# Modulation vectors of the first block: products on ScalarE in place, plain adds on VectorE, the bias row on GpSimd

## The chip, the cores and the metric

The kernel runs on one core of a Trainium2 chip. The core has five engines that matter here: TensorE (PE: matmuls and transposes; PEld is its weight load), VectorE (DVE), ScalarE (ACT), GpSimd (POOL) and SyncE (SP), which only issues DMAs. Each engine takes its instructions from one queue, in order; engines wait for one another by semaphores. The metric is the device time of one execution in microseconds.

## The reference, cut to what matters

The program is two transformer blocks of two layers each, on 512 tokens of width 1024. The change lies in the first block, which has two layers that are modulated by a condition vector `c` (1 x 1024):

```
c_act = silu(c)
for l in range(2):
    mod = c_act @ w_mod[l] + b_mod[l]                 # 1 x 3072, w_mod[l]: 1024 x 3072, f32
    shift, scale, gate = split(mod, 3)                # 1024 each
    h = rms_norm(x, pre_gain[l]) * (1 + scale) + shift
    proj = h @ w_in[l]                                # then attention, retention and gated linear attention (GLA)
    y = concat(attention, retention, gla) @ w_out[l]
    x = x + gate * rms_norm(y, post_gain[l])
```

So each layer needs three vectors of 1024. The scale and shift of layer 0 are needed at once. Its gate is needed only at the end of layer 0, scale and shift of layer 1 at the start of layer 1, and the gate of layer 1 at its end. These four vectors are the ones that the change touches.

## The kernel before, in words

Matmuls of the projections are done in three passes over a weight tile that is split in a rounded and a remaining part: `load_w` (L211 on) loads 128x512 f32 into one of four `raw` buffers by a DMA on SP (L213), ACT casts it (L226), DVE subtracts (L227), and PE multiplies three times (L231 to L233, `mm3`). The four weight buffers are free again when PE has passed. Loads, casts and subtractions of weights thus keep PE's pace.

A vector is made in `mod_steps(l, i)` (L356), a generator that is pulled along beside other work. It treats two halves of 512 columns. For one half it loads the bias (one row, L365) and eight chunks of `w_mod`, 128x512 f32 or 256 KB each (L368), all by SP and all into one ring of two buffers (`rawm`, the bias row included). `mod_acc` (L385) multiplies each chunk by one scalar per partition (column k of `ca`) and adds it up in the tile `acc`, of which there is one: k = 0 is a product (L387) and the addition of the bias row on one partition (L388), k = 1 to 7 are one fused multiply and add each (L390), all on DVE. Then `late`, put off by four steps, lets PE add up the 128 partitions by a matmul with a matrix of ones (L375) and spreads the result over all partitions, and ACT (L377) or DVE (L379, L381) puts it in its place. `acc` is free for the next half when this matmul has read it.

In layer 0, `finish_layer` chains six halves (gate 0, scale 1, shift 1) as `bg`; in layer 1 two (gate 1). `bg` is pulled in the loop over the seven GLA levels (L727), and woven into the GLA chain (L790), the retention chain (L876) and the attention (L1018). The GLA levels: L700 to L704 make the decays `d` of a level on DVE, ACT and POOL, PE multiplies (L669, L679), and DVE selects from the product into `Sg` (L725). The GLA chain: PE multiplies (L781, L783), the norm and gate of its result run on ACT (L543), DVE (L545 to L555) and POOL (L281, L282), PE transposes it (L274), and ACT and DVE split it (L246, L247). Beside it run the projections that `dD` pulls; their rotation is on DVE (L531 to L538) and its transposes on PE (L744).

The first two vectors of layer 0 are made by another function, `mod0` (L416), which calls `mod_acc` too, and which the change leaves alone.

The order in each engine's queue is not the order in the text: a scheduler of the framework places the instructions by its own estimates of times. A change of one operation therefore moves others.

Of the kernel before, what the change touches and what calls it, by code (L numbers as in the profile page):

```python
# [14 lines left out]
OP = mybir.AluOpType  # L15
# [106 lines left out]
def _body(ctx, tc, nc, a, out, stop):  # L122
    V, SC, GP, PE = nc.vector, nc.scalar, nc.gpsimd, nc.tensor
# [30 lines left out]
    def ps_mm():  # L154
        return psum("mm", [128, 512], 4)
# [128 lines left out]
    def bcast_row(dst, row):  # L284
        n = row.shape[-1]
        nc.sync.dma_start(dst, bass.AP(tensor=row.tensor, offset=row.offset, ap=[[0, 128], [1, n]]))
# [22 lines left out]
    def later(steps, fn, key=None):  # L309
        pend.append((clock[0] + steps, fn, key))  # L310
# [31 lines left out]
    def first_block():  # L342
# [5 lines left out]
        ca = fp.tile([128, 8], F32, name="ca")  # L348
# [7 lines left out]
        def mod_steps(l, i):  # L356
            t_ = md.tile([128, D], F32, name=f"mod{i}", bufs=1)
            mod[l][i] = t_
            if i:
                bcast_row(t_, (a["pre_norm_gain"] if i == 1 else a["post_norm_gain"])[l])  # L360
            for n in range(0, D, 512):
                c0 = D * i + n
                acc = md.tile([128, 512], F32, name="acc", bufs=1)
                br = md.tile([128, 512], F32, tag="rawm", name="br", bufs=2)[0:1]
                nc.sync.dma_start(br, a["b_mod"][l:l + 1, c0:c0 + 512])  # L365
                for k in range(8):
                    raw = md.tile([128, 512], F32, tag="rawm", name="rawm", bufs=2)
                    nc.sync.dma_start(raw, a["w_mod"][l, 128 * k:128 * k + 128, c0:c0 + 512])  # L368
                    mod_acc(acc, raw, br, k)
                    if k < 7:  # L370
                        yield 1

                def late(dst=t_[:, n:n + 512], src=acc):
                    ps = ps_mm()
                    PE.matmul(ps, ones, src, start=True, stop=True)  # L375
                    if i == 0:
                        SC.copy(dst, ps)  # L377
                    elif i == 1:
                        V.scalar_tensor_tensor(dst, ps, 1.0, dst, op0=OP.add, op1=OP.mult)  # L379
                    else:  # L380
                        V.tensor_tensor(dst, ps, dst, op=OP.mult)  # L381
                later(RT['mdl'], late, "mod")
                yield 1

        def mod_acc(acc, raw, br, k, eng=V):  # L385
            if k == 0:
                eng.tensor_scalar(acc, raw, ca[:, 0:1], None, op0=OP.mult)  # L387
                eng.tensor_tensor(acc[0:1], acc[0:1], br, op=OP.add)  # L388
            else:
                eng.scalar_tensor_tensor(acc, raw, ca[:, k:k + 1], acc, op0=OP.mult, op1=OP.add)  # L390

        def norm(l, t, x, pl):
# [5 lines left out]
            for n in range(2):  # L398
# [5 lines left out]
        sil = ([fp.tile([128, 512], F32, name=f"sil_a{t}") for t in range(4)],  # L404
               [fp.tile([128, 256], F32, name=f"sil_r{t}") for t in range(4)])
        Ks = [dict(mod=mod[l], sil=sil, mod_steps=mod_steps, norm=norm, md=md) for l in range(2)]
        load_E, mm_E, ev_E = start_layer(0, Ks[0])
        nst = ExitStack()
# [1679 lines left out]
    if SKIP_FIRST:  # L2088
        tst = ExitStack()
        nc.sync.dma_start(con, a["con"])  # L2090
        nc.sync.dma_start(con2, a["con2"])
        tp = pool("tp", stack=tst)
        drain(bias_steps(tp))
        wst = ExitStack()
        more_w("wx", 10, wst, "right")
        E = start_even()
        for t in range(4):
            xt = tp.tile([128, D], F32, name="xt", bufs=2)
            nc.sync.dma_start(xt, xd[t])
            to_T(hT, 0, t, xt, 8)  # L2100
        for t in (3, 2, 1, 0):
            drain(E(t))
        wst.close()
        tst.close()
    else:
        first_block()
# [61 lines left out]
```

## Time and profile before

| | |
|---|---|
| runs of the kernel | 1941.02, 1931.21, 1941.77 us; median 1941.02 |
| profiled execution | 1936.26 us, of which the span of the trace is 1934.5 |
| mean granted TensorE clock in it | 0.992 of full speed |
| PE busy | 1874.2 us, 97% of the span |
| DVE, ACT, POOL busy | 1251.6, 828.1, 260.1 us (65%, 43%, 13%) |
| DMA | 218.76 MB, 113 GB/s in the mean |

All times below are of this one profiled execution. Busy time of an engine counts its instructions, waits left out; idle time of an engine counts only where another engine waits for it. In rows of single instructions the first number is the start in microseconds from the begin of the span, the second the duration, and the brackets hold how long the engine stood idle just before and for which instruction or DMA it waited. A row can hold several like instructions in sequence (x2, x3). PE executes a matmul of f32 in two records. The granted clock is a share of full speed (2.4 GHz; the lower level, 1.2 GHz, is 0.5).

### The profile page before, as it was taken

What the parts mean: (1) busy time and instruction counts of PE and PEld (TensorE: products, weight loads), DVE (VectorE), ACT (ScalarE), POOL (GpSimd) and SP (SyncE); (2) the same over time, 40 slices, a digit from 0 to 9 for tenths busy, and PEclk for the clock granted to TensorE, in tenths of its full rate; (3) what the DMA queues carried; (4) which work ended last, traced back from release to release, by engine and by line L of the source; (5) the groups of instructions that cost most, each with busy time, mean ns of one, the idle gap of its engine ahead of it and who ended that gap; (6) DMA issues with size and microseconds to landing.
All of it is one profiled execution on the core that took longest, in us unless ns stands there. A gap on an engine that the chain in (4) does not pass through costs nothing.

```text
span 1934.5 us, 29305 instructions
## 1 busy us (share of the span) xinstructions
PE 1874.2 (97%) x10144; PEld 1518.6 (79%) x10144; DVE 1251.6 (65%) x3060; ACT 828.1 (43%) x1840; POOL 260.1 (13%) x380
## 2 busy tenths in 40 slices
PE   7899899999999999999999999999999999999997
PEld 4777687877888888868888888788778888888886
DVE  5697886485775244686675674755776776756646
ACT  2432354433463344453443443244665544434341
POOL 3011101012101000101020020101441200200101
PEclk9999999999999999999999999999999999999999
DMA  8535524226124233403373362363114033733632
GB/s 278 173 89 165 150 86 137 86 84 183 44 94 157 73 106 121 153 12 116 117 155 99 91 149 72 117 188 91 42 29 148 24 133 112 154 97 96 134 88 82
DMA packets 139784, 218.76 MB, mean 113 GB/s; under 512 B 21633, under 2 KB 53747, under 8 KB 139636
## 3 DMA queue, kind: packets, MB, share of 16 engines
q1 hardware_dynamic: 130420, 200.11, 33.6%
q0 software_dynamic: 9216, 16.78, 5.2%
q8 instruction: 80, 1.31, 0.3%
q14 instruction: 68, 0.56, 0.1%
HBM read 207.20 MB, written 14.09 MB: 114 GB/s over the span
## 4 chain that ended last, share of the span: by engine, by line
PE 65%; DVE 7%; issue 6%; POOL 3%; DMA 2%; ACT 1%; POOLq 0%; DVEq 0%; SPq 0%; ACTq 0%
PE mm L1060 10%; PE mm L1062 10%; PE mm L1061 9%; PE mm L231 6%; PE mm L233 6%; PE mm L232 6%; PE t L1095 1%; PE o L1547 1%; PE o L1549 1%; PE o L1548 1%; DMA bq<-in_ffn_w_down_dram 1%; PE mm L1547 1%; PE mm L1549 1%; PE mm L1548 1%; PE t L274 1%
## 5 line engine op out<-in xcount | busy, mean ns | idle before, releaser
L227 DVE TENSOR_TENSOR w<-raw,w 128x512 fp32r<-128x512 f32 (+4 forms) x496 | 307.5, 638 | 140.1 <-ACT w L226 138.4
L226 ACT CAST w<-raw 128x512 fp32r<-128x512 f32 (+4 forms) x504 | 284.5, 575 | 239.8 <-PE mm L233 55.9
L1060 PE MATMUL mm<-hT,w 128*128 128x512 f32 x920 | 366.6, 399 | 0.2
L1062 PE MATMUL mm<-hT,w 128*128 128x512 f32 x920 | 361.6, 394 | 0.1
L1061 PE MATMUL mm<-hT,w 128*128 128x512 f32 x920 | 360.7, 392 | 0.0
L231 PE MATMUL mm<-w,hT 128*128 128x512 f32 (+3 forms) x704 | 278.3, 396 | 1.4 <-ACT hT L243 1.3
L233 PE MATMUL mm<-w,hT 128*128 128x512 f32 (+3 forms) x704 | 262.5, 373 | 0.4 <-DVE hT L244 0.4
L232 PE MATMUL mm<-w,hT 128*128 128x512 f32 (+3 forms) x704 | 261.0, 371 | 0.1
L1060 PEld LDWEIGHTS mm<-hT,w 128*128 128x128 f32 x920 | 172.9, 188 | 39.7 <-ACT w L226 1.8
L1062 PEld LDWEIGHTS mm<-hT,w 128*128 128x128 f32 x920 | 172.7, 188 | 39.4 <-DVE w L227 1.3
L1061 PEld LDWEIGHTS mm<-hT,w 128*128 128x128 f32 x920 | 172.9, 188 | 35.2
L231 PEld LDWEIGHTS mm<-w,hT 128*128 128x128 f32 x704 | 138.9, 198 | 31.0 <-issue 6.5
L233 PEld LDWEIGHTS mm<-w,hT 128*128 128x128 f32 x704 | 138.8, 197 | 21.9 <-DVE hT L244 1.3
L232 PEld LDWEIGHTS mm<-w,hT 128*128 128x128 f32 x704 | 139.4, 198 | 16.8 <-issue 2.0
L1525 POOL DMA_DIRECT2D bq<-in_ffn_w_down_dram x64 | 56.6, 1280 | 413.0 <-DVE w L244 401.7
L1576 DVE SCALAR_TENSOR_TENSOR g<-mm,cw,g 128x511 f32<-128x511 f32 x44 | 33.0, 749 | 108.5 <-ACT g L1575 108.4
L243 ACT CAST w<-bq 128x512 fp32r<-128x512 f32 x112 | 69.0, 621 | 65.1 <-DMA bq<-in_ffn_w_down_dram 20.2
L1090 ACT ACTIVATE E<-E,nm 128x128 f32<-128x128 f32 (+3 forms) x128 | 71.6, 560 | 45.0 <-DVE nm L1089 42.3
L244 DVE TENSOR_TENSOR w<-bq,w 128x512 fp32r<-128x512 f32 x112 | 75.5, 689 | 15.4 <-ACT w L243 14.8
L1582 DVE TENSOR_TENSOR ge<-ge,mm 128x512 f32<-128x512 f32 x44 | 30.1, 685 | 67.6 <-PE mm L1062 67.5
L1575 ACT ACTIVATE g<-mm,cw 128x512 f32<-128x512 f32 x44 | 34.2, 777 | 79.6 <-PE mm L1062 63.1
L1085 DVE COPY pT<-t 128x512 f32<-128x512 f32 (+3 forms) x84 | 43.0, 512 | 37.8 <-PE t L1280 23.3
(472 smaller groups left out, 3458.3 us busy)
## 6 DMA issues: line engine op xcount, KB each, us to landing
raw<-in_ffn_w_up_dram SPq DMA_DIRECT2D x160, 256.0 KB
rawm<-in_w_mod_dram SPq DMA_DIRECT2D x96, 256.0 KB
raw<-in_w_in_dram SPq DMA_DIRECT2D x80, 256.0 KB
bq<-in_ffn_w_down_dram POOLq DMA_DIRECT2D x64, 256.0 KB, 7.7
raw<-in_ev_w_in_dram SPq DMA_DIRECT2D x48, 256.0 KB
bq<-in_ffn_w_down_dram SPq DMA_DIRECT2D x48, 256.0 KB
raw<-in_w_out_dram SPq DMA_DIRECT2D x32, 256.0 KB
raw<-in_ffn_w_down_dram SPq DMA_DIRECT2D x24, 256.0 KB
```

Source lines behind the costliest of these rows:

```text
L226: SC.copy(hi, r)
L227: (eng or V).tensor_tensor(lo, r, hi.bitcast(F32), op=OP.subtract)
L231: PE.matmul(ps, hi, w[:, 0, w0:w0 + n], start=first, stop=False)
L232: PE.matmul(ps, hi, w[:, 1, w0:w0 + n], start=False, stop=False)
L233: PE.matmul(ps, lo, w[:, 0, w0:w0 + n], start=False, stop=last)
L243: SC.copy(hi, ps)
L244: V.tensor_tensor(lo, ps, hi.bitcast(F32), op=OP.subtract)
L1060: PE.matmul(ps, wh, hi, start=k == ks[0], stop=False)
L1061: PE.matmul(ps, wh, lo, start=False, stop=False)
L1062: PE.matmul(ps, wl, hi, start=False, stop=k == ks[-1])
L1090: SC.activation(E, E, AF.Exp, scale=scale, bias=nm, accum_out=den)
L1525: GP.dma_start(bufs[name, p], src[then](p), accum_op=OP.add)
```

## The change

`mod_steps` calls a new function, `mod_acc_split`. For k = 0 ACT multiplies the chunk into `acc`, and POOL adds the bias row to its first partition. For k = 1 to 7 ACT multiplies the chunk in place, in its load buffer, and DVE adds it to `acc`. Buffers, loads and the final matmul are the same. `mod_acc` stays for `mod0`.

```diff
-                    mod_acc(acc, raw, br, k)
+                    mod_acc_split(acc, raw, br, k)
...
+        def mod_acc_split(acc, raw, br, k):
+            if k == 0:
+                SC.mul(acc, raw, ca[:, 0:1])
+                GP.tensor_tensor(acc[0:1], acc[0:1], br, op=OP.add)
+            else:
+                SC.mul(raw, raw, ca[:, k:k + 1])
+                V.tensor_tensor(acc, acc, raw, op=OP.add)
```

In the changed kernel all lines from L392 of the old one on have a number that is 8 higher; L387, L388, L390 and L391 are the four operations of the new function there.

The scheduler moves work at several places. On SP, at the beginning of the third half of layer 0 (h3), the queue of the kernel before reads (`br` is the bias row, `rawm` a chunk of `w_mod`, `raw` a weight tile of the projection):

```order
L365 DMA br<-in_b_mod_dram 1x512
L368 DMA rawm<-in_w_mod_dram 128x512
L213 DMA raw<-in_w_in_dram 128x512 x2
L368 DMA rawm<-in_w_mod_dram 128x512 x2
L213 DMA raw<-in_w_in_dram 128x512 x3
L368 DMA rawm<-in_w_mod_dram 128x512 x2
```

and that of the changed kernel:

```order
L365 DMA br<-in_b_mod_dram 1x512
L213 DMA raw<-in_w_in_dram 128x512 x3
L368 DMA rawm<-in_w_mod_dram 128x512
L213 DMA raw<-in_w_in_dram 128x512 x3
L368 DMA rawm<-in_w_mod_dram 128x512 x2
L213 DMA raw<-in_w_in_dram 128x512 x2
```

The first chunk has moved behind three weight loads, the second behind six.

On ACT, in the fourth half (h4), beside the end of the GLA chain, the kernel before has (L246 is the copy of a transposed GLA result, L745 that of a transposed key of the retention):

```order
L246 ACTIVATE yT<-t,ggain 128x2x128
L226 CAST w<-raw 128x512 x4
L246 ACTIVATE yT<-t,ggain 128x2x128
L745 COPY rkT<-t 128x2x128 x2
L226 CAST w<-raw 128x512 x4
```

and the changed kernel (L753 is the old L745):

```order
L387 ACTIVATE acc<-rawm,ca 128x512
L390 ACTIVATE rawm<-rawm,ca 128x512 x2
L246 ACTIVATE yT<-t,ggain 128x2x128
L226 CAST w<-raw 128x512 x4
L246 ACTIVATE yT<-t,ggain 128x2x128
L390 ACTIVATE rawm<-rawm,ca 128x512 x2
L753 COPY rkT<-t 128x2x128
```

The products of k = 0 to 2 stand ahead of the copies and casts, those of k = 3 and 4 behind them. At the end of the second half (h2), the product of k = 7 stands behind four casts in the same way.

On PE, the L375 of h3 has in the kernel before two of four L783 of a GLA result ahead of it:

```order
L274 MATMUL t<-con,ng 128x128 x2
L781 MATMUL o<-smk_1551,qe 128x256
L783 MATMUL o<-v_589,Sg 128x64 x2
L375 MATMUL mm<-acc,ones 128x512
L231 MATMUL mm<-w,hT 128x512
```

and in the changed kernel all of the GLA results and a transposed key (L789, L791 and L752 are the old L781, L783 and L744):

```order
L274 MATMUL t<-con,ng 128x128 x2
L789 MATMUL o<-smk_1571,qe 128x256
L791 MATMUL o<-v_589,Sg 128x64 x4
L789 MATMUL o<-smk_1572,qe 128x256
L274 MATMUL t<-con,ng 128x128 x2
L791 MATMUL o<-v_590,Sg 128x64 x4
L752 MATMUL t<-con,rk_1485 128x128 x2
L375 MATMUL mm<-acc,ones 128x512
```

Eleven short instructions have moved ahead of L375. The L375 of h2 has moved in the same way, behind 18 matmuls of 256 columns (and two transposes) that followed it; that of h4 keeps its place.

## Rows read from the trace of the kernel before

**Rows 1.** The page, first part: busy us, share of the span, instructions.
```profile
PE 1874.2 (97%) x10144; PEld 1518.6 (79%) x10144; DVE 1251.6 (65%) x3060; ACT 828.1 (43%) x1840; POOL 260.1 (13%) x380
```

**Rows 2.** PE's waits in 100 to 432 us: us in total, times, longest.
```profile
PE mm L669 <- DVE Sg L725: 3.0, 4, 0.9
PE mm L375 <- DVE acc L390: 2.1, 2, 1.5
PE mm L679 <- DVE Sg L725: 1.8, 2, 0.9
```

**Rows 3.** Busy us by stretch: PE, PEld, DVE, ACT, POOL; clock, DMA share, GB/s.
```profile
105.00:143.00 38.00, 35.66 (x354) 29.08 (x352) 35.59 (x76) 12.97 (x33) 6.22 (x8) 1.00 0.36 102
...
165.00:187.00 22.00, 20.13 (x94) 15.23 (x94) 16.80 (x42) 6.31 (x13) 2.40 (x4) 0.89 0.39 115
```

**Rows 4.** The tile acc, 60 to 440 us: ns min/median/max, first and last start.
```profile
L390 DVE SCALAR_TENSOR_TENSOR acc<-rawm,ca,acc x56: 729/748/1673, 80.3 to 428.1; 128x512 f32<-128x512 f32 x56
...
L387 DVE TENSOR_SCALAR acc<-rawm,ca x8: 475/482/488, 76.9 to 412.9; 128x512 f32<-128x512 f32 x8
L388 DVE TENSOR_TENSOR acc<-acc,br x8: 669/670/680, 77.4 to 413.9; 1x512 f32<-1x512 f32 x8
```

**Rows 5.** Single lines over the whole span, same columns: nearest operations.
```profile
L227 DVE TENSOR_TENSOR w<-raw,w x496: 397/683/1214, 56.5 to 1906.2; 128x512 fp32r<-128x512 f32 x129, 128x256 fp32r<-128x256 f32 x27, 128x272 fp32r<-128x272 f32 x6, 128x312 fp32r<-128x312 f32 x2
...
L226 ACT CAST w<-raw x504: 388/620/640, 21.1 to 1905.6; 128x512 fp32r<-128x512 f32 x129, 128x256 fp32r<-128x256 f32 x27, 128x272 fp32r<-128x272 f32 x6, 128x312 fp32r<-128x312 f32 x3
...
L1872 ACT ACTIVATE vm<-mm,rk x4: 687/690/692, 1455.7 to 1461.2; 128x512 f32<-128x512 f32 x4
...
L751 POOL TENSOR_TENSOR qe<-qe,qF x2: 1278/1280/1282, 133.6 to 421.2; 128x512 f32<-128x512 f32 x2
```

**Rows 6.** SP's issues in 125 to 190 us: start, us, what is loaded.
```profile
141.28 0.34 SPq L368 DMA_DIRECT2D rawm<-in_w_mod_dram  x1
...
147.00 1.73 SPq L213 DMA_DIRECT2D raw<-in_w_in_dram  x3
...
150.49 3.36 SPq L213 DMA_DIRECT2D raw<-in_w_in_dram  x3
```

**Rows 7.** ACT in 142 to 180 us: start, us, idle before and its releaser.
```profile
142.72 0.62 ACT L226 CAST w<-raw 128x512 fp32r<-128x512 f32 x1 [0.59 <-PE mm L233]
...
176.53 2.73 ACT L226 CAST w<-raw 128x512 fp32r<-128x512 f32 x4 [0.23 <-PE mm L233]
179.17 0.47 ACT L246 ACTIVATE yT<-t,ggain 128x256 fp32r<-128x256 f32 x1
```

**Rows 8.** DVE in 133 to 186 us, same columns.
```profile
133.80 1.60 DVE L390 SCALAR_TENSOR_TENSOR acc<-rawm,ca,acc 128x512 f32<-128x512 f32 x1
...
162.94 0.74 DVE L390 SCALAR_TENSOR_TENSOR acc<-rawm,ca,acc 128x512 f32<-128x512 f32 x1
...
177.27 0.75 DVE L390 SCALAR_TENSOR_TENSOR acc<-rawm,ca,acc 128x512 f32<-128x512 f32 x1
...
180.81 0.75 DVE L390 SCALAR_TENSOR_TENSOR acc<-rawm,ca,acc 128x512 f32<-128x512 f32 x1 [0.21 <-DMA rawm<-in_w_mod_dram]
...
184.38 0.75 DVE L390 SCALAR_TENSOR_TENSOR acc<-rawm,ca,acc 128x512 f32<-128x512 f32 x1 [0.37 <-DMA rawm<-in_w_mod_dram]
```

**Rows 9.** PE in 141 to 186 us, same columns.
```profile
141.43 0.28 PE L232 MATMUL mm<-w,hT 128*128 128x256 f32 x1
141.55 1.02 PE L375 MATMUL mm<-acc,ones 128*128 128x512 f32 x2
...
163.74 2.08 PE L375 MATMUL mm<-acc,ones 128*128 128x512 f32 x2 [1.49 <-DVE acc L390]
...
173.12 1.00 PE L783 MATMUL o<-v,Sg 128*128 128x64 f32 x8
```

**Rows 10.** The tile acc, 184 to 246 us: first and last start.
```profile
L390 DVE SCALAR_TENSOR_TENSOR acc<-rawm,ca,acc x15: 732/746/891, 184.4 to 229.2; 128x512 f32<-128x512 f32 x15
...
L375 PE MATMUL mm<-acc,ones x6: 592/594/697, 185.2 to 244.6; 128*128 128x512 f32 x6
```

## The prediction

> **What bounds the kernel now.** The page's first part comes first: TensorE (PE) is busy 97% of the span, VectorE (DVE) 65%, ScalarE (ACT) 43%, GpSimd (POOL) 13% [rows 1]. So microseconds taken from DVE are worth nothing by themselves; a change pays only where PE stands idle and waits for DVE. The list of PE's waits over 100 to 432 us, where the changed lines run, shows what can be had: L669 and L679 wait for the DVE select L725 (3.0 and 1.8 us in both layers), and L375, the matmul that ends each half of a modulation vector, waits for the last L390 twice, 2.1 us in all [rows 2]. Then the table of stretches: in 105 to 143 us, the seven GLA levels of layer 0, DVE is busy 35.59 of 38 us while ACT has 25 us free. That is the one stretch where DVE is short. In 165 to 187 us DVE has 5 us free and the granted clock is 0.89 [rows 3]. PE had stood idle just before (1.49 us ahead of the L375 at 163.74 [rows 9]), so a longer wait of PE may cost a second time, by a stretch at the lower of its two levels (1.2 GHz).
>
> I number the eight halves h1 to h8 (h1 to h6 in layer 0) and the eight 256 KB chunks of each k0 to k7. A half is a serial loop: two buffers carry the chunks, and the load of k+2 is issued when chunk k has been read. In h4 one sees the turn: L390 of k3 ends at 177.27 + 0.75 = 178.02, k5 starts at 180.81, 2.79 later; k5 ends at 181.56, k7 starts at 184.38, 2.82 later [rows 8]. So a load costs about 2.8 us from free buffer to next use, and whatever lengthens the use of a buffer lengthens the loop.
>
> **The change on the engines.** DVE loses eight L387 at 0.482, eight L388 at 0.670 and 56 L390 at 0.748 [rows 4]: 3.9 + 5.4 + 41.9 = 51.1 us. It gains 56 plain adds of two 128x512 tiles in SBUF, for which L227 stands at 0.683 [rows 5]: 38.2 us. Net 12.9 us less, or 1.6 a half: nearly all of it from k0, only 0.065 from each later chunk. POOL gains eight adds on one row of 512; L388 takes as long on one partition as L227 on 128, so the length of the row sets the time, and L751 gives 1.28 each, 10 us in all [rows 5]. ACT gains 64 products of 128x512 with a pointer to a scale. The trace has no such product out of SBUF; bounds are the plain cast L226 at 0.620 from SBUF and L1872 at 0.690 with a scale from PSUM. I take 0.69, the same kind of instruction: 44 us, for which ACT has room in the mean. No activation-table load is added.
>
> The price is in the loop. A buffer was free 0.75 after its load had landed and DVE came round; now it needs the ACT product (0.69), a hop and the DVE add (0.68), both in order behind whatever stands in their queues. With two buffers, eight chunks make four turns, so 4 x 0.65 = 2.6 us more a half if nothing blocks, and more where the product stands behind ACT work that waits for PE. Stretch by stretch:
>
> GLA levels (h2 in layer 0, h8 in layer 1). L387 and L388 (1.15 us together) leave the queue in which the selects stand, but DVE there waits for loads and exponentials too. Of the 4.8 us that L669 and L679 wait [rows 2] I take half, **-2.4**; bounds 0 and -4.8.
>
> End of h2. PE needs L375 at 141.55 before and finds it ready; the order puts it 18 short matmuls later, whose starts lie 0.12 apart [rows 9], so at about 143.6. But k7's product stands behind four casts that wait for PE, the last at 142.72 + 0.62 = 143.34 [rows 7]; plus 0.69 and 0.68 is 144.7. So **+1.1**; bounds 0 and +2.
>
> h3. In SP's queue k0's load goes from ahead of the first three weight loads to behind them, k1's behind six. Before, k0 was issued at 141.28, two weight loads went out before 147.00, so the third is the first of the row there, and the sixth the first of that at 150.49 [rows 6]. Weight loads wait for free weight buffers, which PE's pace sets, so k0 starts up to 6 us later. From k1 at 150.8: landed 153.6, product and add done 155.0, k3 159.1, k5 163.3, k7 167.5 (each turn 2.8 + 0.69 + 0.68). Before, k7's L390 ended at 162.94 + 0.74 = 163.7 [rows 8]. PE reached that L375 at 163.74 - 1.49 = 162.25 [rows 9]; the new order puts eleven short instructions of the GLA chain ahead of it; four of them (eight records of L783) take 1.00 [rows 9], so I take 2.0 for all. PE gets there at 164.3 and has 2.0 us less to do afterwards: later by 167.5 - 163.7 - 2.0 = **+1.8**; bounds 0 (the weight loads themselves go out earlier, now that fewer modulation loads stand ahead of them) and +4.
>
> h4. On ACT, k3's product stands behind a block that runs in before from 176.53 (four casts, 2.73 us, held by PE) to 179.17 + 0.47 = 179.64 [rows 7]; before, DVE had k3 done at 178.02. Now k3 is done at 179.64 + 0.69 + 0.68 = 181.0, k5 at 181.0 + 2.8 + 1.37 = 185.2, k7 at 189.4, against 185.13 before [rows 8]. L375 keeps its place among PE's matmuls and already waited there (2.1 less 1.49 is 0.6 [rows 2, 9]). So 4.3 us later by itself; PE comes some 1.5 to 3 later too, and I take **+3**; bounds 0 and +4.5.
>
> The others I cost at 0. h1's stall is in another chain; in h5 PE did not wait and has retention work to spare; in h6 the last L390 starts at 229.2 and L375 at 244.2, 15 us of cover [rows 10]; h7 and h8 have theirs moved later with them. If that cover were gone each would pay its 2.6. The clock I also cost at 0: the stretch at 165 to 187 has 0.89 of full speed over 22 us, that is 22 x 0.11 x 2 = 4.8 us at half clock and 2.4 lost [rows 3]; one such stretch may come after h4's longer wait or go after h3's.
>
> Sum: -2.4 + 1.1 + 1.8 + 3 = **+3.5 us** on the profiled execution's 1936.3, so 1939.8. That execution lies 4.8 below the median of the three runs (1941.0) and inside their range (1931.2 to 1941.8); the mean of all four is 1937.6. Counted from that mean, as all cases below, I get 1941.1; I say 1941.
>
> **POOL beside DVE.** The L390 at 133.80 took 1.60 instead of 0.75 [rows 8]; POOL's L751 began at 133.6 and took 1.28 [rows 5]. So an addition on POOL can stretch the DVE operation beside it by 0.85, and eight new ones could give back 8 x 0.85 = 6.8 of the 12.9. The Trainium skill, "SBUF — State Buffer", section "Who interferes with whom", has a rule for this: a DVE instruction with two SBUF inputs contends with a GpSimd instruction that reads SBUF, and the one that came first keeps the port to its end. The row agrees, and by the rule the move of the bias row buys DVE little. The same skill, "ScalarE: Activation LUTs", section "Rules for kernel authors", would leave multiplications on VectorE for their speed; here L1872's 0.690 against L387's 0.482 goes the same way, and what decides is not that but the queue it stands in.
>
> **Rivals.**
> (a) DVE is what counts: all 4.8 us at the selects go, the 2.1 at L375 too, and with them the stretch at the lower clock (2.4). That is -9.3: 1928.3. For it: DVE at 94% in 105 to 143. Against: the adds still need the products, and each later chunk saves DVE only 0.065.
> (b) The slower side: the loop through ACT. If products stand behind PE-held work in every half that PE needs soon (h2, h3, h4, h5), each at its upper bound (2 + 4 + 4.5 + 2.6 = 13.1), with one more stretch at the lower clock (+2.4), and the selects give 2.4 back: +13.1, 1950.7. It decides once k3 or an earlier product of h3 and h4 is later than about 2 us behind its load. Against: PE's delay in one half gives the next half time.
> (c) The bias on POOL: the stretched DVE operations fall into the selects and the -2.4 is not had: +5.9, 1943.5.
> (d) The change does not reach PE at all: loads go out earlier where weight loads moved ahead, all lies under cover: 1937.6.
>
> **Numbers.** Chances: forecast 0.40, (a) 0.14, (b) 0.24, (c) 0.10, (d) 0.12. A measurement of this kernel can tell 0.5% (9.7 us) from no change. Beyond it on the faster side lies half of (a), 0.07, and 0.04 for the edges of the other cases: 0.11. On the slower side lie two thirds of (b), 0.16, and a sixth of the forecast and of (c), 0.09: 0.25. The rest, 0.64, is within. The range runs from (a) to somewhat over (b), 1929 to 1953, as (b) is open upward. The forecast's own range, by the bounds of its terms (-4.8 and +10.5 at most), is 1933 to 1948.
>
> **What would show it.** Right: DVE's total falls by about 13 us (or 6 with the contention) and ACT's rises by 44; PE's waits for L725 shrink to about half; PE's waits at L375 (in the new list) grow from 2.1 to about 8 us, in h2, h3 and h4, with an ACT product behind casts as the last releaser; products at about 0.69 and bias rows at about 1.28. Wrong: L375 waits no longer than before, weight casts starting later for want of their loads with PE waiting behind them, or the stretches at the lower clock deciding by their number alone.

## The result and the profile after

| | before | changed |
|---|---|---|
| median of 5 runs, us | 1941.02 (1931.21 to 1944.37) | 1960.39 (1955.58 to 1968.08) |
| ratio, 95% interval | 1 | 1.0106 (1.0082 to 1.0129) |
| profiled execution, us | 1936.26, clock 0.992 | 1968.08, clock 0.981 |

The change costs 20 us, or 1.1%. The sign of the forecast was right and its size was not: +3.5 us (1941) was forecast, with an upper end of 1953. The profiled execution of the changed kernel is the slowest of its five, with the lowest clock; that of the kernel before lost less to the clock than most. So the two traces lie 31.8 us apart, more than the 20 of the medians. The first part of the page for the changed kernel:

```profile
PE 1890.9 (96%) x10144; PEld 1528.9 (78%) x10144; DVE 1244.2 (63%) x3044; ACT 869.8 (44%) x1904; POOL 272.4 (14%) x388
```

Against [rows 1] DVE has lost 7.4 us of work, ACT has gained 41.7 and POOL 12.3. The relief of DVE that the change was to bring is there. PE is busy 16.7 us longer, though it executes the same number of instructions. The list of PE's waits (here over 100 to 445 us, since the same work takes longer) says where some of the time went; L677, L687 and L733 are L669, L679 and L725 of [rows 2]:

```profile
PE mm L375 <- DVE acc L391: 9.3, 2, 7.6
...
PE mm L677 <- DVE Sg L733: 2.7, 4, 0.8
...
PE t L770 <- POOL kl L766: 1.9, 1, 1.9
...
PE mm L687 <- DVE Sg L733: 0.9, 2, 0.5
```

The waits for the select fell from 3.0 + 1.8 to 2.7 + 0.9, by 1.2 us. The wait at L375 grew from 2.1 to 9.3 us, and a wait for `kl` is new. The stretches show the other half. Columns as in [rows 3]:

```profile
105.00:143.00 38.00, 35.88 (x323) 29.23 (x321) 30.94 (x68) 16.32 (x37) 6.47 (x7) 0.91 0.33 92
...
165.00:187.00 22.00, 18.81 (x90) 14.67 (x89) 13.56 (x36) 9.75 (x19) 4.85 (x7) 0.92 0.33 94
187.00:208.00 21.00, 12.28 (x58) 8.52 (x58) 13.24 (x28) 8.38 (x14) 3.49 (x3) 0.76 0.61 176
```

and the last stretch in the kernel before:

```profile
187.00:208.00 21.00, 19.94 (x113) 15.29 (x113) 16.80 (x44) 5.64 (x14) 6.00 (x9) 1.00 0.62 184
```

DVE has fallen from 35.6 to 30.9 us of the first 38, in part because fewer of its instructions fall into the stretch (68 for 76). The granted clock is 0.91 there, where it was 1.00, but this is not tied to the loss: experiment 1, as slow as the change, has 1.00 in that stretch, and experiment 7, faster than the kernel before, has 0.91. From 143 to 165 it is 0.84 (0.96 before), from 165 to 187 it is 0.92 (0.89 before). From 187 to 208, where it was 1.00 before, it is 0.76, with PE busy for only 12.3 of 21 us; this one comes back in experiments 1 and 5, which have the same long wait of PE.

How much is waiting and how much is clock can be worked out from the list of runs, which gives span and clock of each. The five runs of the changed kernel have clocks of 0.981, 0.987, 0.984, 0.986 and 0.982; span times clock, the span as it would be if all of it ran at full speed, is 1927.7 us in the mean, and the mean span 1959.1, so 31.4 us are lost at the lower level. I call the first the full-speed work; waits of PE count in it. In the 71 runs of the kernel before that stand beside the experiments, the mean span is 1939.7 and 21.8 are lost; a line through these runs gives 0.65 us of span for each microsecond lost (correlation 0.82). That it is less than 1 would fit a part of the lower level falling where PE waits anyway, which is not shown. So of the 19.4 us between the mean spans, 9.6 more are lost to the clock, worth 6 (at 0.65) to 9.6 by estimate, and the other 10 to 13 are waits. The two lists of PE's waits agree with that: all their lines together come to 27.5 us against 17.9, 9.6 more. (The profiled execution of before, with 0.992, lost 15.5.)

**The loop.** The chunk's tile `acc`, min, median and max in ns, then what its instructions waited for (us, times):

```profile
L391 DVE TENSOR_TENSOR acc<-acc,rawm x56: 673/690/1210, 79.8 to 452.5; 128x512 f32<-128x512 f32 x56
...
L387 ACT ACTIVATE acc<-rawm,ca x8: 721/722/725, 75.4 to 434.6; 128x512 f32<-128x512 f32 x8
L388 POOL TENSOR_TENSOR acc<-acc,br x8: 1263/1272/1287, 76.2 to 435.4; 1x512 f32<-1x512 f32 x8
...
  ACT rawm L390: 16.6, 18
  DMA rawm<-in_w_mod_dram: 12.7, 3
```

and the group of products from the second chunk on, in 100 to 460 us (busy us and mean ns, then idle time of ACT just before them and its releasers):

```profile
L390 ACT ACTIVATE rawm<-rawm,ca 128x512 f32<-128x512 f32 x49 | 35.2, 721 | 37.0 <-DMA rawm<-in_w_mod_dram 32.7 <-DVE qrot L546 2.2 <-DVE Sg L733 1.8
```

An ACT product out of SBUF takes 0.72, a little over the 0.69 taken from [rows 5]. The adds take 0.69 in the median, but 0.715 in the mean of this window; some run beside POOL, as one row below shows. Before 49 products ACT waits 33 us for chunks to land: the loop runs at the pace of its loads and buffers. One sees the pace on SP, where seven of h2's chunk loads are issued in a row (start, us, count). Before:

```profile
125.93 11.62 SPq L368 DMA_DIRECT2D rawm<-in_w_mod_dram  x7
```

and in the changed kernel, with the first loads of h3 behind:

```profile
128.36 13.47 SPq L368 DMA_DIRECT2D rawm<-in_w_mod_dram  x7
...
146.24 0.33 SPq L368 DMA_DIRECT2D rawm<-in_w_mod_dram  x1
...
153.76 0.80 SPq L368 DMA_DIRECT2D rawm<-in_w_mod_dram  x2
```

Seven loads take 13.47 us instead of 11.62: three turns more or less of 0.6 us each. That is the 0.65 a turn of the prediction. Then h3's k0 is issued at 146.24, five microseconds later than in [rows 6], and k1 and k2 at 153.76.

**The place in the queue.** ACT in h4 (start, us, idle before and its releaser; L387 and L390 here are the products):

```profile
182.44 0.72 ACT L390 ACTIVATE rawm<-rawm,ca 128x512 f32<-128x512 f32 x1 [0.98 <-DMA rawm<-in_w_mod_dram]
...
183.80 2.70 ACT L226 CAST w<-raw 128x512 fp32r<-128x512 f32 x4 [0.23 <-PE mm L233]
186.41 0.47 ACT L246 ACTIVATE yT<-t,ggain 128x256 fp32r<-128x256 f32 x1
186.78 1.32 ACT L390 ACTIVATE rawm<-rawm,ca 128x512 f32<-128x512 f32 x2
...
192.01 0.72 ACT L390 ACTIVATE rawm<-rawm,ca 128x512 f32<-128x512 f32 x1
...
196.40 0.72 ACT L390 ACTIVATE rawm<-rawm,ca 128x512 f32<-128x512 f32 x1 [0.85 <-DMA rawm<-in_w_mod_dram]
```

DVE's adds of k3, k5 and k7 in the same half:

```profile
187.91 0.69 DVE L391 TENSOR_TENSOR acc<-acc,rawm 128x512 f32<-128x512 f32 x1
...
192.76 0.69 DVE L391 TENSOR_TENSOR acc<-acc,rawm 128x512 f32<-128x512 f32 x1 [0.83 <-ACT rawm L390]
...
197.75 1.21 DVE L391 TENSOR_TENSOR acc<-acc,rawm 128x512 f32<-128x512 f32 x1
```

This is the chain that was forecast: k3's product waits behind four casts and a copy until 186.78, and its add ends at 188.60; k5's product comes at 192.01, k7's at 196.40, each a load and a hop later. The last add, 1.21 long instead of 0.69, runs beside an operation of the retention on POOL (197.31 to 198.41). PE's side of it, and two instructions by which the delay can be read:

```profile
174.53 1.51 PE L375 MATMUL mm<-acc,ones 128*128 128x512 f32 x2 [1.77 <-DVE acc L391]
...
199.10 2.05 PE L375 MATMUL mm<-acc,ones 128*128 128x512 f32 x2 [7.55 <-DVE acc L391]
201.08 1.23 PE L814 MATMUL mm<-rqT,rkT 64*128 64x128 f32 x8
...
425.03 1.76 PE L677 MATMUL mm<-d 32*128 32x128 f32 x16 [0.75 <-DVE Sg L733]
```

and the same in the kernel before, for the last three:

```profile
185.19 1.12 PE L375 MATMUL mm<-acc,ones 128*128 128x512 f32 x2 [0.62 <-DVE acc L390]
186.25 0.72 PE L806 MATMUL mm<-rqT,rkT 64*128 64x128 f32 x8
...
406.10 1.76 PE L669 MATMUL mm<-d 32*128 32x128 f32 x16 [0.77 <-DVE Sg L725]
```

L375 of h4 waits 7.55 us instead of 0.62. L814 (the old L806) behind it starts at 201.08 instead of 186.25, 14.8 us late; the first waiting matmul of layer 1's levels starts at 425.03 instead of 406.10, 18.9 us late. The span ends 31.8 us late. The first matmul of the second block (L1060, now L1068) starts at 652.37 instead of 628.57, 23.8 us late; so the last 8.0 arise in the second block, which the change does not touch (from 600 to 900 us the granted clock is 0.98, before it was 1.00).

### The profile page after: what moved, and what is told of

Same layout as the page of the kernel before. It is cut to its first block, busy times and chain, and to the rows that moved or that the text cites. A ratio compares the mean times of both kernels' runs of the same rounds, so it can differ in the third digit from the quotient of the medians.

```text
span 1966.3 us, 29370 instructions
## 1 busy us (share of the span) xinstructions
PE 1890.9 (96%) x10144; PEld 1528.9 (78%) x10144; DVE 1244.2 (63%) x3044; ACT 869.8 (44%) x1904; POOL 272.4 (14%) x388
## 4 chain that ended last, share of the span: by engine, by line
PE 65%; DVE 7%; DMA 4%; POOL 3%; ACT 2%; issue 2%; POOLq 0%; DVEq 0%; SPq 0%; ACTq 0%
PE mm L1068 10%; PE mm L1070 10%; PE mm L1069 10%; PE mm L231 6%; PE mm L233 6%; PE mm L232 6%; DMA bq<-in_ffn_w_down_dram 2%; PE t L1103 1%; PE o L1555 1%; PE o L1557 1%; PE o L1556 1%; DVE w L227 1%; PE t L274 1%; PE o L1954 1%; POOL bq L1533 1%
## 5 line engine op out<-in xcount | busy, mean ns | idle before, releaser
L1068 PE MATMUL mm<-hT,w 128*128 128x512 f32 x920 | 366.4, 398 | 0.3 <-ACT w L226 0.2
L1068 PEld LDWEIGHTS mm<-hT,w 128*128 128x128 f32 x920 | 172.8, 188 | 39.7 <-ACT w L226 1.9
L231 PEld LDWEIGHTS mm<-w,hT 128*128 128x128 f32 x704 | 141.3, 201 | 33.4 <-issue 9.0
L233 PEld LDWEIGHTS mm<-w,hT 128*128 128x128 f32 x704 | 140.6, 200 | 22.3 <-DVE hT L244 1.7
L232 PEld LDWEIGHTS mm<-w,hT 128*128 128x128 f32 x704 | 141.6, 201 | 17.6 <-issue 1.5
```

The lines of the kernel that those rows point to most:

```text
L231: PE.matmul(ps, hi, w[:, 0, w0:w0 + n], start=first, stop=False)
L232: PE.matmul(ps, hi, w[:, 1, w0:w0 + n], start=False, stop=False)
L233: PE.matmul(ps, lo, w[:, 0, w0:w0 + n], start=False, stop=last)
L1068: PE.matmul(ps, wh, hi, start=k == ks[0], stop=False)
```

## The experiments

Theory A: with two buffers, product and add in series hold each chunk longer; the loop of a half becomes longer, PE waits and the clock falls more often. Theory B: the bias row on POOL does it. Theory C: not the series but ACT's load, or its queue by itself, does it. Ratios are against the kernel before on the same chip in the same session.

**1. Bias row back on DVE.**
```diff
-                GP.tensor_tensor(acc[0:1], acc[0:1], br, op=OP.add)
+                V.tensor_tensor(acc[0:1], acc[0:1], br, op=OP.add)
```


> The products stay on ACT in place, the bias row goes back to DVE. Theory A (the products of k1 to k7 in ACT's queue make the loop long, the changed order follows from them; some 8 us of waits and, through more stretches at the lower clock, some 10 more): about as slow as the changed kernel, ratio 1.007 to 1.011, L375 of h4 still waits over 5 us. Theory B (the bias row on POOL holds the second buffer and stands behind other POOL work): ratio 1.004 or less, and L375 of h4 waits under 3 us.

1.0117 (1.0084 to 1.0151), 1961.2 us. The waits of PE:

```profile
PE mm L375 <- DVE acc L391: 8.8, 2, 7.4
...
PE mm L677 <- DVE Sg L733: 1.6, 3, 0.6
...
PE t L770 <- POOL kl L766: 1.9, 1, 1.9
```

No difference from the change that can be told: B falls. The longest wait, that of h4, is 7.4 us with the row on DVE and 7.6 with the row on POOL.

**2. Only the bias row on POOL.**
```diff
-                SC.mul(acc, raw, ca[:, 0:1])
+                V.tensor_scalar(acc, raw, ca[:, 0:1], None, op0=OP.mult)
                 GP.tensor_tensor(acc[0:1], acc[0:1], br, op=OP.add)
...
-                SC.mul(raw, raw, ca[:, k:k + 1])
-                V.tensor_tensor(acc, acc, raw, op=OP.add)
+                V.scalar_tensor_tensor(acc, raw, ca[:, k:k + 1], acc, op0=OP.mult, op1=OP.add)
```


> All products and fused adds back on DVE, only the bias row on POOL. Theory A: as the kernel before, ratio 0.997 to 1.002, stretches at the lower clock as before (granted clock 0.991 to 0.993). Theory B: 1.005 or more.

1.0013 (0.9990 to 1.0035). No difference that can be told; B falls from this side too. The clock of its ten runs goes from 0.986 to 0.994, wider than I expected.

**3. Only the first chunk split.**
```diff
                 GP.tensor_tensor(acc[0:1], acc[0:1], br, op=OP.add)
...
-                SC.mul(raw, raw, ca[:, k:k + 1])
-                V.tensor_tensor(acc, acc, raw, op=OP.add)
+                V.scalar_tensor_tensor(acc, raw, ca[:, k:k + 1], acc, op0=OP.mult, op1=OP.add)
```


> Only k0 is changed (product on ACT, bias row on POOL); k1 to k7 are fused on DVE as before. It has 1.15 of the 1.6 us that DVE saves in each half. Theory A: 0.996 to 1.002, PE's waits for L725 a bit shorter. Theory B: 1.004 or more.

1.0005 (0.9984 to 1.0027). Most of DVE's relief is in this kernel (1.15 of 1.6 us a half), and it brings nothing; PE's waits for the select are not shorter either, 3.2 + 1.8 us in its list. So the loss is in the products of k1 to k7, and the relief of DVE is worth little by itself.

**4. A second reader on ACT.**
```diff
                     mod_acc(acc, raw, br, k)
+                    idle = md.tile([128, 512], mybir.dt.bfloat16, name="idle", bufs=1)
+                    SC.mul(idle, raw, ca[:, k:k + 1])
```


> The kernel before, with a second reader of each chunk: ACT multiplies every chunk into a tile that nobody reads (bf16, same number of elements). DVE's part and the sum are unchanged; a buffer comes free when both have read it. Theory A as a queue on ACT that holds buffers: slower, 1.004 to 1.010, the loads late as in the changed kernel, though no product is in series with the add. Theory C (it is the series ACT to DVE that costs, not ACT's queue): 1.003 or less.

1.0016 (0.9997 to 1.0035). (The expectation names the theories otherwise: its theory C, the series, is theory A above, and its theory A, the queue on ACT, is theory C above.) The same number of products stands in ACT's queue, and it costs at most some 7 us by its interval, a third of the loss. So ACT's load is not it: theory C above falls in that form. Beside DVE's fused operation, the product does not lengthen a turn by itself; the seven loads of h2 take 11.74 us, as before the change (11.62):

```profile
128.01 11.74 SPq L368 DMA_DIRECT2D rawm<-in_w_mod_dram  x7
```

**5. Split only in h3 and h4.**
```diff
-                    mod_acc_split(acc, raw, br, k)
+                    (mod_acc_split if i == 1 else mod_acc)(acc, raw, br, k)
```


> The split of the change only in h3 and h4 (scale of layer 1, made beside the GLA chain of layer 0); the other six halves as before, bias row included. If h3 and h4 carry the loss (L375 there waits 1.8 and 7.6 us in the changed kernel, and stretches at the lower clock follow): ratio 1.005 to 1.009. If the loss is spread over all halves by the longer loop: 1.003 or less.

1.0038 (1.0018 to 1.0058), between my two cases. The long wait is there:

```profile
PE mm L375 <- DVE acc L391: 8.0, 1, 8.0
```

**6. Split everywhere else.**
```diff
-                    mod_acc_split(acc, raw, br, k)
+                    (mod_acc if i == 1 else mod_acc_split)(acc, raw, br, k)
```


> The split in h1, h2, h5 to h8; h3 and h4 as before. If h3 and h4 carry the loss: 1.000 to 1.004 (the wait for POOL's kl at L770, 1.9 us in each layer, stays). If spread: 1.007 or more.

1.0072 (1.0048 to 1.0096). PE waits no more at L375 than before (L398 is the fused add here), and more at other places, `kl` among them:

```profile
PE t L770 <- POOL kl L766: 3.8, 2, 1.9
...
PE o L837 <- DVE rot L540: 2.8, 1, 2.8
PE t L752 <- DVE rk L546: 2.2, 1, 2.2
...
PE mm L375 <- DVE acc L398: 1.5, 1, 1.5
```

0.38% and 0.72% make up the 1.06%, within their intervals: the halves add. So do the two kinds of cost. Against the runs of the kernel before beside them, 5 has 3.4 us more of full-speed work (span times clock) and loses 3.6 more to the clock, 6 has 7.8 and 7.0; the sums are 11.2 and 10.6, and the change itself has 9.8 and 9.6. A third of the loss comes from h3 and h4, where L375 waits 8 us; two thirds come from h1, h2 and h5 to h8, where PE hardly waits at L375 in the list. That the wait at L375 is the loss, as I had thought, is a third of the truth.

**7. Three buffers.** In 7, 8, 9, 10 and 12 room is made by one `rS` buffer less (three for four) and by `th0` in a small shared tile; in 7, 8 and 12 two later tiles of the same ring (`oh`, `rows`) have three buffers too. Only the lines on the ring of the vectors are shown.
```diff
-                br = md.tile([128, 512], F32, tag="rawm", name="br", bufs=2)[0:1]
+                br = md.tile([128, 512], F32, tag="rawm", name="br", bufs=3)[0:1]
...
-                    raw = md.tile([128, 512], F32, tag="rawm", name="rawm", bufs=2)
+                    raw = md.tile([128, 512], F32, tag="rawm", name="rawm", bufs=3)
```


> The changed kernel with three buffers for the chunks instead of two (room made by one rS buffer less in the retention and a small tile put elsewhere). If the two buffers make the loop (each turn has a load of 2.8 us, a product and an add in series), the third takes it away: ratio to the kernel before 0.998 to 1.003. If the place of the products in ACT's queue decides: 1.007 or more.

0.9946 (0.9927 to 0.9965), 1933.4 us. The same split that cost 20 us is now 0.5% faster than the kernel before. Six of h2's loads on SP:

```profile
127.17 7.79 SPq L368 DMA_DIRECT2D rawm<-in_w_mod_dram  x6
```

That is 1.3 us a load, against 1.9 in the changed kernel (13.47 for seven) and 1.7 in the kernel before. Two of the stretches, with a clock of 0.91 and 1.00 where the change has 0.91 and 0.76:

```profile
105.00:143.00 38.00, 35.10 (x319) 28.58 (x318) 31.58 (x69) 15.65 (x35) 6.65 (x8) 0.91 0.36 105
187.00:208.00 21.00, 20.85 (x125) 16.56 (x124) 17.03 (x49) 9.67 (x23) 7.72 (x10) 1.00 0.47 140
```

**8. Three buffers in the kernel before** (the same edit on that kernel).

> The control for three buffers: the kernel before with three buffers, the same room made. 0.997 to 1.001: PE waits only 2.1 us at L375, so there is little to win; what it gains or loses is to be taken from the run with the split.

0.9933 (0.9902 to 0.9964), 1928.8 us: the fastest of all. I had expected nothing of it, because PE waited so little at L375. Its six runs lose 12 us to the clock in the mean (span 1926.8, span times clock 1914.6), against 23 in the 21 runs of the kernel before beside them: the kernel before itself was paying for its two buffers. Between 7 and 8, both with three buffers, the split now costs 0.13% by their ratios, within their intervals.

**9. The product in a tile of its own**, two buffers for chunks.
```diff
-                SC.mul(raw, raw, ca[:, k:k + 1])
-                V.tensor_tensor(acc, acc, raw, op=OP.add)
+                pr = md.tile([128, 512], F32, name="pr", bufs=1)
+                SC.mul(pr, raw, ca[:, k:k + 1])
+                V.tensor_tensor(acc, acc, pr, op=OP.add)
```


> The split with two buffers for chunks as in the changed kernel, but the product goes to a third tile of its own instead of in place, so a load buffer is free after ACT's product (0.72 after its load) and not after DVE's add. The room is that of the third buffer. If it is the buffer held through product and add in series that costs: ratio to before 0.995 to 1.002. If the place of the products in ACT's queue costs (k3 of h4 behind four casts): 1.006 or more, for a load buffer still waits for ACT.

0.9969 (0.9951 to 0.9986), 1936.0 us. Seven loads of h2 on SP:

```profile
127.45 10.86 SPq L368 DMA_DIRECT2D rawm<-in_w_mod_dram  x7
```

10.86 us instead of 13.47, and less than the 11.62 of before. PE's waits at the selects and at L375:

```profile
PE mm L678 <- DVE Sg L734: 2.4, 4, 0.9
PE mm L375 <- DVE acc L392: 2.3, 2, 1.2
```

This is the sharpest test: products on ACT, adds on DVE, the bias row on POOL, eight halves as in the change, and besides the room only this is different, that a load buffer is free after the product instead of after the add. The loss is gone. The scheduler's order is another one here as well, though: in h2 all of `kl`'s exponentials stand ahead of the casts, and in h4 no product stands behind four of them.

**10. Control: only the room made.**
```diff
-        th0 = fp.tile([128, 8], F32, name="th0")
+        th0 = sm.tile([128, 8], F32, name="rp")
...
-                        s_ = rp.tile([128, 2, 128], F32, name="rS", bufs=4)
+                        s_ = rp.tile([128, 2, 128], F32, name="rS", bufs=3)
```


> Control: the kernel before with two buffers and only the room made (one rS buffer less, th0 in a small shared tile). If the gain of 0.993 with three buffers comes from the buffers, 0.998 to 1.002 here; if from these edits, about 0.993.

0.9978 (0.9963 to 0.9994). A little faster than expected, by the edge of its interval. So a part of 7 to 9, up to 0.2%, is not the buffers: against this control the tile of its own (9) is no faster, and three buffers (8) are 0.45% faster (0.1 to 0.8 by the two intervals). What 7, 9, 10 and 12 gain against the kernel before is all in the clock: their full-speed work is 0 to 1 us more than that of the kernel before beside them, and they lose 4 to 10 us less at the lower level. Only 8 has less work as well, by 2.8 us.

**11. L375 put off.**
```diff
-          l0=7, lv=3.3, mdl=4, rm=9, ...
+          l0=7, lv=3.3, mdl=9, rm=9, ...
```


> The changed kernel with its L375 put off by nine steps instead of four in the order of the program. If PE's waits at L375 are the loss: 1.000 to 1.005. If the long loop is (acc is held longer, the next half begins later): 1.006 to 1.013.

1.0130 (1.0101 to 1.0158), 1968.0 us: no gain, rather worse. But the wait did not go away with it:

```profile
PE mm L375 <- DVE acc L391: 7.1, 2, 6.5
```

A later L375 holds `acc` longer, and the next half begins later: h3's k0 is issued at 155.76 instead of 146.24. So this run does not tell the wait from the loop. Its full-speed work is that of the change (1927.5 against 1927.7 us), and what it is longer by is lost to the clock (38.8 against 31.4).

**12. First chunk split, three buffers** (the edits of 3 and 7).

> Three buffers, only k0 split (ACT product, POOL bias row), k1 to k7 fused on DVE. It has most of DVE's saving without a series in seven of eight chunks. 0.990 to 0.994, at or a little under the kernel before with three buffers (0.9933); if the bias row on POOL or the hop costs there too, 0.995 or more.

0.9968 (0.9949 to 0.9988), 1933.9 us: worse than the first case and within the second (0.995 or more, the bias row or the hop costs). The intervals of 8 and 12 overlap, so that such a cost exists is not shown. No better than 8 is what the run does show: the relief of DVE does not pay here either.

Each of these kernels gets an order of its own from the scheduler, which knows the buffers. So a shorter loop and a better order come together (in 7 and 9 no product stands behind four casts in h4). How much of the loss was the order and how much the length of a turn in the same order was not separated.

## Why the prediction was wrong

**What held.** DVE is no bound, and its relief does not pay (3, 12). The sums of work: ACT +44 forecast, +41.7 measured; POOL +10 and +12.3; DVE -13 or -6 with the contention, -7.4 measured (in part by luck, see the end of this section). The turn of the loop, longer by 0.65 forecast and 0.62 measured in h2. The mechanism at the end of the chain: k3 of h4 behind the casts. PE's waits at L375 grew to 9.3 us where about 8 were named as the sign of being right, though in h3 and h4 only; so most signs came true, and the time did not.

**The terms near L375.** At the selects -2.4 was forecast and the list has -1.2, which is no more than this list differs between kernels with the loop on DVE (4.0 us in experiment 2, 5.0 in 3, 4.8 in the kernel before). In h3 I had PE wait 3.2 (167.5 less 164.3), and it waits 1.77. In h2 I had it wait 1.1 at L375; it waits 1.9 instead a step ahead, at L770 for `kl`: the last of `kl`'s exponentials on ACT now stands behind the product of k7 and four casts. ACT before,

```profile
138.20 0.99 ACT L756 ACTIVATE kl<-b 128x128 f32<-128x128 f32 x3 [4.39 <-PE mm L679]
```

and in the changed kernel, with PE's transpose of `kl`:

```profile
143.72 1.14 ACT L226 CAST w<-raw 128x512 fp32r<-128x512 f32 x2 [0.41 <-PE mm L233]
144.77 0.72 ACT L390 ACTIVATE rawm<-rawm,ca 128x512 f32<-128x512 f32 x1
...
145.79 0.39 ACT L764 ACTIVATE kl<-b 128x128 f32<-128x128 f32 x1
...
147.36 0.44 PE L770 MATMUL t<-con,kl 128*128 128x128 f32 x2 [1.89 <-POOL kl L766]
```

In h4 I worked out 4.3, took 3, and it is 6.9 (7.55 less 0.62). Two things were missing there, and the first is the larger. The half begins late, its first product at 177.18 against L387 at 167.39 before; and the second buffer is that of the bias row, which POOL reads from here on:

```profile
178.44 1.27 POOL L388 TENSOR_TENSOR acc<-acc,br 1x512 f32<-1x512 f32 x1
```

until 179.71. The chunk that takes its buffer is used at 182.44, 2.7 later. This second thing is worth little: with the row on DVE (experiment 1) the wait is 7.4 instead of 7.6. Summed up, these terms are -1.2, +1.9, +0.3 (1.77 less 1.49, in h3) and +6.9: 7.9 where I had 3.5.

**The step that failed first is "The others I cost at 0".** I priced each half by PE's cover at its L375, and found cover for h1 and h5 to h8. Experiment 6 has two thirds of the loss in h1, h2 and h5 to h8, with no more wait at L375 than before. In mean spans, h3 and h4 cost 7.0 us (experiment 5), where +4.8 was forecast; all the rest costs 14.8 (experiment 6), where -2.4 + 1.1 + 0 = -1.3 was forecast. Experiment 6 does not part h2, priced at +1.1, from the five halves at 0; its list has 1.9 us at `kl` in layer 0, beside h2, and 1.9 in layer 1, beside the last halves, neither of which was in the sum. What the runs show in place of the cover: PE meets the longer loop not only at L375. At `kl` it can be followed row by row through ACT's queue; at a transposed key (L752) and a result of the retention (L837) the list of experiment 6 has 2.2 and 2.8 us, and the way there was not followed. Rival (b) had the mechanism, the loop through ACT, but priced it at L375 too, and its upper bounds came to 1950.7. Rival (c) fell with experiments 1 and 2. Rival (a) fell as well: PE waits 1.2 us less at the selects. So did (d), that PE is not reached at all.

**The second is "The clock I also cost at 0".** It is 6 to 9.6 of the 19.4 us, by the estimate above. I had the row for it, 0.89 after an idle PE [rows 3], and let coming and going stretches cancel, although three of the four other terms of the sum said that PE would idle more. From 187 to 208 alone the clock is 0.76 where it was 1.00, 21 x 0.24 = 5.0 us of full-speed work, a part of it while PE waits.

What stays open: why stretches at the lower clock appear also where the program is unchanged, in the second block, and which of the small waits makes each of them; and how much of the loss in h1, h2 and h5 to h8 belongs to each half.

On POOL beside DVE: the add at 197.75, with two inputs in SBUF, took 1.21 us instead of 0.69 beside a POOL operation. That agrees with the rule of the Trainium skill, "SBUF — State Buffer", section "Who interferes with whom", by which a DVE instruction with two SBUF inputs contends with a GpSimd instruction that reads SBUF. But the POOL operation there is none of the new ones, and the 6.8 us of the prediction for eight bias rows was too much: with the row back on DVE (experiment 1) DVE's total is 1247.1 us, 2.9 more than in the change, where eight rows at 0.670 make 5.4. So the rows on POOL stretch DVE's work by some 2.5 us at most, by this estimate, and the rest of what DVE's total lacks against 12.9 has another source, which stays open. Experiment 1 shows no effect of it at the end of the span.

## What to carry to other kernels

When one operation in a ring of few buffers is split over two engines, ask first how long the buffer is held, and by whom: in place, it is held through both queues. Give the product a tile of its own or the ring a third buffer before moving any work; here that turned a loss of 1.1% into a gain of 0.3 to 0.5%, and the third buffer without any split gave 0.7% (of each, the room made for it may be 0.2). Price a longer loop by everything that shares its queues, not by the one wait at its end. And where a change lets PE idle more often, the lower clock that follows belongs into the sum with its sign.

## What the runs showed of the hardware

The lower clock is not the same from run to run of one kernel. 71 runs of the kernel before have spans from 1931.0 to 1949.2 us, and the full-speed work lost to the lower level goes from 11.6 to 35.1 us; with a correlation of 0.82 that goes with about two thirds of the variance. With a third buffer less is lost: nine runs of experiment 7, with times between 1930.3 and 1935.6 us, lose 13.5 in the mean, six of experiment 8 lose 12.2 and ten of experiment 12 lose 14.5, against 21.8.

One stretch at the lower level comes with one wait. From 187 to 208 us the profiled clock is 0.76 in the three kernels whose PE waits 7.4 to 8.0 us at the L375 of h4 (the change, 1 and 5), 0.88 in experiment 11, whose longest wait there is 6.5, and 0.92 to 1.00 in the other ten. From 105 to 143 us the same profiles have 0.85 to 1.00, without regard to which kernel is slow.

POOL adds a row of 512 on one partition in 1.27 us, as long as its product of two tiles of 512 on 128 partitions takes (1.28 in [rows 5]).
